# Feed-forward products of a two-layer trunk by Strassen's scheme over pairs of tiles

## The chip, the cores and the metric

The kernel runs on one core of one Trainium2 chip. TensorE (PE) multiplies matrices, VectorE (DVE), ScalarE (ACT) and GpSimd (POOL) work elementwise, and DMA queues, issued from SyncE (SP) or from GpSimd, move data between HBM and the on-chip memory SBUF. Products land in PSUM. The metric is device time in microseconds (us) of one execution.

## The reference

The reference is the trunk of a streaming encoder: 512 frames with 16 learned meta tokens in front, 1024 features, float32. Layer 0 is multi-scale retention, layer 1 multi-head latent attention with a shared compressed key and value; each layer ends with a dense feed-forward of hidden width 2816, with a norm ahead of each part and a residual addition behind it.

```python
def swiglu(hn, w1, w3, w2):
    return (jax.nn.silu(hn @ w1) * (hn @ w3)) @ w2

    for layer in range(DEPTH):
        hn = rmsnorm(h, norm_mix_g[layer])
...
        h = h + swiglu(rmsnorm(h, norm_ffn_g[layer]), ffn_w1[layer], ffn_w3[layer], ffn_w2[layer])
    return rmsnorm(h, final_g)[:, PAD + N_META:]
```

## The kernel before

Activations stay transposed: 128 features on the partitions of a tile, tokens along the free axis. The residual stream is eight tiles h0 to h7. A float32 product is three passes over operands split into an upper half (a cast on ACT) and a lower half (a subtraction on DVE); `split` (L212, L208) does it for weights as well as for activations, and `split_scaled` (L224, L225) together with a norm's gain.

The program runs in stages: retention (0 to 466 us), the feed-forward of layer 0 over 528 tokens (to 854), attention (to 1126), the feed-forward of layer 1 over 512 frames (to 1494), and an end. In a feed-forward (`ffn`), `gemm` walks over 44 tiles of 128 columns of w1 and w3 in turn, eight contraction tiles each, in two halves of 22; after each second tile `evac` scales both products by the norm's 1/rms, takes silu (L638), multiplies and splits the hidden tile. After each half, `gemm` multiplies eight columns of w2 with its eleven hidden tiles, and `add` adds the product to h. In the second half `add` also calls `prep`, which makes the next stage's operand from that h and sums its squares while the next tile's matmuls run. In layer 1 the second half of w2 is done by `finish`, for one half of the frames and then for the other, with the final norm and the output.

All operands live in one pool of 57 slots, and weights come through three buffers of raw, upper and lower halves (`wp`); PSUM has four buffers of two banks (1024 columns). On every engine instructions run in program order; the framework's scheduler has set that order from the code, and semaphores make each wait for its producers. GpSimd only issues transfers.

## Time and profile before

| what | before |
|---|---|
| median of 3 runs | 1505.89 us (1505.42 to 1507.55) |
| span of the profiled execution | 1505.8 us |
| its own time beside the span | not listed apart; the span lies within the runs' times |
| PE busy | 1486.9 us (99%) |
| DVE busy | 846.7 us (56%) |
| ACT busy | 571.0 us (38%) |
| POOL busy | 20.9 us (1%) |
| feed-forward stages | 466 to 854 and 1126 to 1494 us |

A busy share is that engine's own time over the span. Matmuls are pipelined, so a matmul's listed duration is longer than its distance to the next one; the chain of waits divides its length by their number.

### The profile page before, as it was taken

To read this page: it belongs to the slowest core of one execution; us is meant where nothing else is said; L and a number is where in the kernel's file an instruction comes from. 1 tells how busy PE (TensorE), PEld (TensorE's weight loads), DVE (VectorE), ACT (ScalarE), POOL (GpSimd) and SP (SyncE) were. 2 spreads that over 40 slices of the span, in tenths; PEclk is the share of its full clock that TensorE was granted. 3 is DMA by queue.
4 is the path that set the end of the run, shared out by engine and by line. 5 is a ranking of instruction groups with operands and counts; after the bars stand their busy time and mean duration, and the time that the engine had idled before them with its cause. 6 is when DMAs were issued, how large, how long until landed. Compare 5 with 4: busy or idle time off the path is not lost.

```text
span 1505.8 us, 24568 instructions
## 1 busy us (share of the span) xinstructions
PE 1486.9 (99%) x10450; PEld 1392.0 (92%) x10450; DVE 846.7 (56%) x1286; ACT 571.0 (38%) x946; POOL 20.9 (1%) x44
## 2 busy tenths in 40 slices
PE   8999999999999999999999999999999999999997
PEld 8999999999999999999999998889888888888896
DVE  7665565565577444234445667677885443344464
ACT  5452342342345222123224435666464222222251
POOL 1000000000000000000000000110000000000000
PEclk9999999999999999999999999999999999999998
DMA  5213213213212222332323422321113223323251
GB/s 202 88 47 111 80 46 110 80 48 109 70 58 94 89 88 70 96 112 86 95 67 87 139 84 80 103 67 67 57 44 111 98 81 88 112 98 98 81 160 57
DMA packets 43022, 133.91 MB, mean 89 GB/s; under 512 B 5136, under 2 KB 8720, under 8 KB 42912
## 3 DMA queue, kind: packets, MB, share of 16 engines
q1 hardware_dynamic: 40464, 125.98, 25.7%
q0 software_dynamic: 2448, 6.36, 1.5%
q8 instruction: 82, 1.34, 0.4%
q14 instruction: 28, 0.23, 0.0%
HBM read 128.91 MB, written 2.10 MB: 87 GB/s over the span
## 4 chain that ended last, share of the span: by engine, by line
PE 96%; DVE 1%; ACT 1%; DMA 0%; issue 0%; SPq 0%; DVEq 0%; ACTq 0%
PE ps L246 47%; PE ps L248 28%; PE ps L483 7%; PE ps L915 4%; PE ps L566 2%; PE ps L106 2%; PE ps L524 2%; PE ps L147 1%; PE ps L489 1%; PE ps L491 1%; PE ps L132 1%; PE ps L296 1%; DVE s L208 1%; ACT s L864 0%; DMA s<-w_q 0%; PE ps L567 0%
## 5 line engine op out<-in xcount | busy, mean ns | idle before, releaser
L246 PE MATMUL ps<-s,whi 128*128 128x264 f32 x3904 | 638.2, 285 | 6.5 <-ACT s L224 6.4
L246 PEld LDWEIGHTS ps<-s,whi 128*128 128x128 f32 x3904 | 543.4, 189 | 8.0 <-ACT s L224 6.8
L212 ACT CAST whi<-raw 128x1024 fp32r<-128x1024 f32 (+5 forms) x270 | 246.1, 917 | 652.3 <-PE ps L246 310.2
L246 PE MATMUL ps<-s,wlo 128*128 128x264 f32 x1952 | 398.4, 286 | 0.0
L248 PE MATMUL ps<-s,whi 128*128 128x512 f32 x1248 | 391.9, 395 | 0.5 <-DVE s L208 0.4
L208 DVE TENSOR_TENSOR wlo<-raw,whi 128x1024 fp32r<-128x1024 f32 (+5 forms) x270 | 284.3, 1056 | 107.2 <-ACT whi L212 104.7
L246 PEld LDWEIGHTS ps<-s,wlo 128*128 128x128 f32 x1952 | 303.8, 189 | 0.0
L248 PEld LDWEIGHTS ps<-s,whi 128*128 128x128 f32 x1248 | 232.4, 188 | 54.0 <-DVE s L208 1.0
L248 PE MATMUL ps<-s,wlo 128*128 128x512 f32 x624 | 244.8, 392 | 0.0
L208 DVE TENSOR_TENSOR t<-ps,s 128x528 f32<-128x528 f32 (+1 forms) x120 | 83.0, 700 | 279.8 <-PE ps L246 162.0
L248 PEld LDWEIGHTS ps<-s,wlo 128*128 128x128 f32 x624 | 117.1, 188 | 27.0
L208 DVE TENSOR_TENSOR h<-ps,h 128x528 f32<-128x528 f32 (+2 forms) x100 | 64.9, 653 | 93.3 <-PE ps L246 64.3
L483 PE MATMUL ps<-whi,s 128*128 128x256 f32 x640 | 116.0, 281 | 0.0
L208 DVE TENSOR_TENSOR s<-ps,s 128x256 fp32r<-128x256 f32 (+4 forms) x107 | 59.4, 571 | 89.9 <-ACT s L212 51.5
L483 PEld LDWEIGHTS ps<-whi,s 128*128 128x128 f32 x640 | 99.2, 189 | 0.2
L483 PE MATMUL ps<-wlo,s 128*128 128x256 f32 x320 | 89.7, 280 | 0.0
L483 PEld LDWEIGHTS ps<-wlo,s 128*128 128x128 f32 x320 | 60.4, 189 | 0.0
L212 ACT CAST s<-t 128x528 fp32r<-128x528 f32 (+2 forms) x68 | 40.2, 603 | 48.2 <-DVE t L208 39.4
L208 DVE TENSOR_TENSOR s<-s,s 128x528 fp32r<-128x528 f32 (+4 forms) x85 | 53.7, 657 | 4.9 <-ACT s L212 4.7
L212 ACT CAST s<-ps 128x256 fp32r<-128x256 f32 (+2 forms) x72 | 31.7, 445 | 61.0 <-PE ps L483 50.1
L208 DVE TENSOR_TENSOR s<-t,s 128x528 fp32r<-128x528 f32 (+2 forms) x68 | 44.5, 664 | 8.6 <-ACT s L212 8.4
L212 ACT CAST s<-s 128x528 fp32r<-128x528 f32 (+2 forms) x57 | 32.8, 584 | 39.8 <-DVE s L208 37.3
(140 smaller groups left out, 1105.1 us busy)
## 6 DMA issues: line engine op xcount, KB each, us to landing
raw<-w SPq DMA_DIRECT2D x99, 512.0 KB, 3.5
raw<-w SPq DMA_DIRECT2D x24, 384.0 KB, 3.1
raw<-w_v SPq DMA_DIRECT2D x16, 512.0 KB, 3.8
raw<-w_g SPq DMA_DIRECT2D x16, 512.0 KB, 3.4
raw<-w_ro SPq DMA_DIRECT2D x16, 512.0 KB, 3.4
raw<-w SPq DMA_DIRECT2D x24, 320.0 KB, 2.9
raw<-w_mo SPq DMA_DIRECT2D x8, 512.0 KB, 3.4
raw<-w_q SPq DMA_DIRECT2D x7, 512.0 KB, 4.2
```

Of the source, the lines that this page charges most:

```text
L106: nc.tensor.matmul(out, x[:, qs], y[:, cs], start=t == 0, stop=t == 4 and not masked)
L132: nc.tensor.transpose(pt[:, j * P : (j + 1) * P], p[:, META + j * P : META + (j + 1) * P], k.ident)
L147: nc.tensor.matmul(po[:, q0:SEQ], x, y, start=j == 0 and t == 0, stop=False)
L208: self.nc.vector.tensor_tensor(out=out, in0=a, in1=b, op=op)
L212: self.nc.scalar.copy(out=hi, in_=src)
L246: mm(ps[:, h * 512 : h * 512 + HT], w[p], x[q][:, h * HT : (h + 1) * HT], start=s, stop=e)
L248: mm(ps[:, :SEQ], w[p], x[q], start=s, stop=e)
L296: self.nc.tensor.matmul(ps[:, h * 512 : h * 512 + w], one, z[:, h * w : (h + 1) * w], start=i == 0, stop=i == len(acc) - 1)
L483: mm(ps[:, :256], x[k][p][:, c], w[k][q], start=k == 0 and i == 0, stop=k == last and i == 2)
L524: nc.tensor.matmul(ps[:n, half * 512 : half * 512 + HT], k[d][p][:, t0 : t0 + n], q[d][s][:, half * HT : (half + 1) * HT], start=i == 0, s ...
L566: mm(out, v[j][p][:, c], s[:, c0 : c0 + HT], start=j == 0 and i == 0, stop=False)
L915: nc.tensor.matmul(ps[:, :n], p, q, start=k == 0 and i == 0, stop=k == len(x) - 1 and i == 2)
```

## The change

Both feed-forwards are computed by the Strassen-Winograd scheme: two output tiles by two halves of the tokens, over pairs of contraction tiles, take seven products in place of eight. `quad` makes four output blocks, in four one-bank PSUM tiles, from seven factors of the weight and seven operands of the activation.

`factors` brings the four blocks of a weight and makes the sums: s3 and s1 by a plain transfer into SBUF followed by an accumulating one from GpSimd's queue, s2 and its second value by additions on DVE. All seven factors are split on ACT and DVE, 512 columns at a time. `operands` makes four differences on GpSimd and splits seven operands. The product of silu and gate is on GpSimd too. In `ffn`, a weight of w13 now has tile m of w1 and tile m of w3 side by side (22 up quads), and w2 comes in parts of 3, 3, 3 and 2 pairs of hidden tiles with four down quads each. Ahead of the down quads of the first three parts, one up quad of the next part is put.

The pools are opened and closed by stage, so that a stage's memory is free for the next. The preparation for attention now stands at the start of `mla`, that for layer 1's feed-forward after attention's pools are shut, and `finish` is replaced by the same down quads and a final norm over the whole frame. Weights of the other stages are split in pieces of 512. The order of some work between heads in attention is changed, too.

```diff
-SLOTS = 57
+WP = 512
+EW = 4 * HT
+RET_SLOTS = 45
+MLA_SLOTS = 53
+PARTS = (3, 3, 3, 2)
...
         self.retention()
-        self.ffn(0, True, self.prep_mla)
+        self.shut("pp", "yp")
+        self.hp = self.pool("hp", "right", 4)
+        self.ffn(0, True)
+        self.shut("hp", "wp")
+        self.weight_pool(2 * WP, 3, 6)
+        self.metas("mm", 4)
+        self.pp = self.pool("pp", bufs=4, space=PSUM)
+        self.sp = self.pool("sp", bufs=MLA_SLOTS)
         self.mla()
-        self.ffn(1, False, None)
+        self.shut("pp", "sp", "mm", "wp")
+        self.weight_pool(3 * WP, 2, 5)
+        self.xp = self.pool("xp", bufs=4)
+        self.hp = self.pool("hp", "right", 4)
+        for k in range(KD):
+            self.prep_ffn(1, k)
+        self.ffn(1, False)
...
     def prep_ffn(self, layer, k):
+        full = layer == 0
+        n = T if full else SEQ
+        v = self.h[k] if full else self.h[k][:, META:]
         if k == 0:
-            self.acc, self.x = self.slot(), []
-        self.x.append(self.prep(k, f"ffn{layer}", self.acc, layer == 0))
+            self.x = []
+        if k % 2 == 0:
+            self.vv = self.wide()[:, : 2 * n].rearrange("p (i c) -> p i c", i=2)
+        self.nc.scalar.activation(out=self.vv[:, k % 2], in_=v, func=AF.Copy, scale=self.g(f"ffn{layer}", k))
+        self.square_add(self.acc[:, :n], v, k == 0)
+        if k % 2:
+            self.x.append(self.operands(self.xp, self.vv, n // 2))
...
+    def operands(self, pool, vv, w):
+        nc = self.nc
+        add = nc.gpsimd.tensor_tensor
+        xp = pool.tile([P, 7, 2, HT], F32R, tag="xp", name=self.name("xp"))
+        tm = self.wide()[:, : 4 * w].rearrange("p (j c) -> p j c", j=4)
+        (b11, b12), (b21, b22) = ((vv[:, i, :w], vv[:, i, w : 2 * w]) for i in range(2))
+        add(out=tm[:, 2], in0=b12, in1=b11, op=ALU.subtract)
+        add(out=tm[:, 0], in0=b12, in1=b22, op=ALU.subtract)
+        add(out=tm[:, 1], in0=b22, in1=tm[:, 2], op=ALU.subtract)
+        add(out=tm[:, 3], in0=b21, in1=tm[:, 1], op=ALU.subtract)
+        self.split(xp[:, 0:2, 0, :w], xp[:, 0:2, 1, :w], vv[:, :, :w])
+        self.split(xp[:, 3:7, 0, :w], xp[:, 3:7, 1, :w], tm)
+        self.split_scaled(xp[:, 2, 0, :w], xp[:, 2, 1, :w], b22, -1.0)
+        return xp
+    def factors(self, src, n):
+        nc = self.nc
+        raw = self.raw()
+        s1, s2, s3 = (self.wp.tile([P, WP], F32, tag=t, name=self.name(t), bufs=1)[:, :n] for t in ("s1", "s2", "s3"))
+        nc.sync.dma_start(out=s3, in_=src[:, 3 * n : 4 * n])
+        nc.sync.dma_start(out=raw[:, : 3 * n], in_=src[:, : 3 * n])
+        nc.sync.dma_start(out=s1, in_=src[:, 3 * n : 4 * n])
+        nc.gpsimd.dma_start(out=s3, in_=src[:, :n], accum_op=ALU.add)
+        nc.gpsimd.dma_start(out=s1, in_=src[:, 2 * n : 3 * n], accum_op=ALU.add)
+        a11, a12, a22 = (raw[:, i * n : (i + 1) * n] for i in range(3))
+        for j, z in enumerate((a11, s3, s2, s1, a12, a22, s2)):
+            if j == 2:
+                self.tt(s2, s1, a11, ALU.add)
+            if j == 6:
+                self.tt(s2, s2, a12, ALU.add)
+            hi, lo = (t[:, :n] for t in self.ring())
+            self.split(hi, lo, z)
+            yield hi, lo
+    def quad(self, src, xs, w):
+        nc = self.nc
+        n = len(xs) * P
+        fac = self.factors(src, n)
+        ev = self.wide()[:, : 4 * w].rearrange("p (j c) -> p j c", j=4)
+        q1, u2, u3 = ev[:, 0], ev[:, 1], ev[:, 2]
+        def product(bank, j, first, last):
+            wt = next(fac)
+            for k, xp in enumerate(xs):
+                c = slice(k * P, (k + 1) * P)
+                for i, (p, q) in enumerate(((0, 0), (0, 1), (1, 0))):
+                    nc.tensor.matmul(bank[:, :w], wt[p][:, c], xp[:, j, q, :w], start=first and k == 0 and i == 0,
+                                     stop=last and k == len(xs) - 1 and i == 2, skip_group_check=True)
+        a, b, c, d = (self.bank() for _ in range(4))
+        product(a, 0, True, False)
+        nc.scalar.copy(out=q1, in_=a[:, :w])
+        product(d, 3, True, False)
+        product(b, 4, True, True)
+        self.tt(u2, b[:, :w], q1, ALU.subtract)
+        self.tt(u3, d[:, :w], u2, ALU.add)
+        product(c, 5, True, False)
+        c2 = self.temp()[:, : 2 * w]
+        self.tt(c2[:, w:], c[:, :w], u3, ALU.add)
+        product(a, 1, False, True)
+        product(d, 6, False, True)
+        self.tt(c2[:, :w], d[:, :w], u2, ALU.add)
+        product(c, 2, False, True)
+        self.tt(u3, c[:, :w], u2, ALU.add)
+        return a[:, :w], u3, c2
...
+        def up(m):
+            nonlocal vv
+            c11, c12, c2 = self.quad(a[f"w13_{layer}"][m], x, w)
+            if m == 0:
+                rstd()
+            c1 = self.temp()[:, :n]
+            self.tt(c1[:, :w], c11, r[:, :w], ALU.mult)
+            nc.vector.scalar_tensor_tensor(out=c1[:, w:], in0=c12, scalar=-1.0, in1=r[:, w:n], op0=ALU.mult, op1=ALU.mult)
+            self.tt(c2, c2, r[:, :n], ALU.mult)
+            nc.scalar.activation(out=c1, in_=c1, func=AF.Silu)
             if m % 2 == 0:
...
+                vv = self.wide()[:, : 2 * n].rearrange("p (i c) -> p i c", i=2)
+            nc.gpsimd.tensor_tensor(out=vv[:, m % 2], in0=c1, in1=c2, op=ALU.mult)
+            if m % 2:
+                hid.append(self.operands(self.hp, vv, w))
+        def down(part, xs, last):
+            for q in range(KD // 2):
+                c11, c12, c2 = self.quad(a[f"w2_{layer}_{part}"][q], xs, w)
+                h1, h2 = (z if full else z[:, META:] for z in self.h[2 * q : 2 * q + 2])
+                self.tt(h1[:, :w], c11, h1[:, :w], ALU.add)
+                self.tt(h1[:, w:], h1[:, w:], c12, ALU.subtract)
+                self.tt(h2, h2, c2, ALU.add)
+                if last and not full:
+                    for m in (2 * q, 2 * q + 1):
+                        self.square_add(acc, self.h[m][:, META:], m == 0)
+        m = 0
+        for part, size in enumerate(PARTS):
+            end = 2 * sum(PARTS[: part + 1])
+            ahead = 1 if part < len(PARTS) - 1 else 0
+            while m < end + ahead:
+                up(m)
+                m += 1
+            xs, hid[:] = hid[:size], hid[size:]
+            last = part == len(PARTS) - 1
+            if last:
+                self.shut("xp")
+            down(part, xs, last)
+        if not full:
+            rstd()
+            for k in range(KD):
+                hv = self.h[k][:, META:]
+                nc.vector.scalar_tensor_tensor(out=hv, in0=hv, scalar=self.g("final", k), in1=r[:, :n],
+                                               op0=ALU.mult, op1=ALU.mult)
+                nc.sync.dma_start(out=a["outT"][:, k], in_=hv)
+        self.shut("bk")
...
     def mla(self):
         nc, a = self.nc, self.a
+        for k in range(KD):
+            self.prep_mla(k)
         acc, xkv, xq = self.parted(self.acc, True), self.x, self.xq
-        r = self.slot()
+        r = self.r
...
-                if MH // 2 - 1 in pairs:
-                    self.prep_ffn(1, m)
```

The order of instructions, at three places. First GpSimd. Before, it holds nothing but DMA issues; these are the last of retention's decay tables and the first transfers of attention (ktrig, qtrig), with both feed-forward halves of layer 0 between decm_475 and s_1093.

```order
L415 DMA decm_321_2538<-decay_meta 16x528
L413 DMA dec_474_3796<-decay 128x656
L415 DMA decm_475_3798<-decay_meta 16x528
L666 DMA s_1093_9361<-ktrig 128x528
L669 DMA s_1094_9363<-qtrig 128x512
```

In the change, two up quads of layer 0's feed-forward stand on GpSimd as follows (s3 and s1 are weight sums, L806 the product of silu and gate into a pair's buffer e_884, L713 to L716 the differences for operand pair e_911).

```order
L731 DMA s3_920_6238<-w13_0 128x512
L806 TENSOR_TENSOR e_884_6075<-t_883_6070,t_876_6017 128x528
L713 TENSOR_TENSOR e_911_6219<-e_884_6075 128x264
L732 DMA s1_918_6236<-w13_0 128x512
L731 DMA s3_946_6380<-w13_0 128x512
L806 TENSOR_TENSOR e_884_6075<-t_909_6212,t_902_6159 128x528
L714 TENSOR_TENSOR e_911_6219<-e_884_6075 128x264
L715 TENSOR_TENSOR e_911_6219<-e_884_6075,e_911_6219 128x264
L716 TENSOR_TENSOR e_911_6219<-e_884_6075,e_911_6219 128x264
L732 DMA s1_944_6378<-w13_0 128x512
L731 DMA s3_973_6533<-w13_0 128x512
```

What moved: the products and differences are new there, and each accumulating transfer for s1 (L732) is issued only behind them. Next DVE, in the middle of layer 0's feed-forward. Before, it is the evacuation of one pair of product tiles (ps) by r (s_672), between lower halves of weights (wlo):

```order
L208 TENSOR_TENSOR t_882_7539<-ps_874_7429,s_672_5341 128x528
L208 TENSOR_TENSOR wlo_893_7607<-raw_891_7605,whi_892_7606 128x1024
L208 TENSOR_TENSOR t_883_7540<-ps_878_7484,s_672_5341 128x528
L208 TENSOR_TENSOR t_883_7540<-t_883_7540,t_882_7539 128x528
L208 TENSOR_TENSOR wlo_901_7672<-raw_899_7670,whi_900_7671 128x1024
L208 TENSOR_TENSOR s_885_7546<-t_883_7540,s_884_7545 128x528
L208 TENSOR_TENSOR t_894_7659<-ps_886_7549,s_672_5341 128x528
```

In the change, a stretch of the same stage (bk are PSUM banks, e_885 and e_912 combinations, c1 is t_909, xp_910 the operands of one pair):

```order
L245 TENSOR_TENSOR e_885_6077<-bk_888_6080,e_885_6077 128x264
L245 TENSOR_TENSOR wlo_928_6297<-s1_918_6236,whi_927_6296 128x512
L801 SCALAR_TENSOR_TENSOR t_909_6212<-e_885_6077,r_83 128x264
L245 TENSOR_TENSOR wlo_931_6315<-raw_917_6235,whi_930_6314 128x512
L245 TENSOR_TENSOR wlo_933_6331<-raw_917_6235,whi_932_6330 128x512
L245 TENSOR_TENSOR s2_919_6237<-s2_919_6237,raw_917_6235 128x512
L245 TENSOR_TENSOR xp_910_6218<-e_884_6075,xp_910_6218 128x2x264
L262 SCALAR_TENSOR_TENSOR xp_910_6218<-e_884_6075,xp_910_6218 128x264
L245 TENSOR_TENSOR e_912_6230<-bk_914_6232,e_912_6230 128x264
L245 TENSOR_TENSOR wlo_935_6349<-s2_919_6237,whi_934_6348 128x512
L245 TENSOR_TENSOR xp_910_6218<-e_911_6219,xp_910_6218 128x4x264
L245 TENSOR_TENSOR e_912_6230<-bk_916_6234,e_912_6230 128x264
```

What moved: combinations of banks and the subtractions for operand pairs now stand among the lower halves of weights, which have become halves of 512. Last DVE where layer 0's feed-forward meets attention. Before, the last two tiles' additions to h6 and h7, each followed by its operands (s_1074, s_1077, s_1086, s_1089) and its sum of squares (s_1001):

```order
L208 TENSOR_TENSOR h6_79<-ps_1066_9174,h6_79 128x528
L208 TENSOR_TENSOR wlo_1101_9380<-raw_1099_9378,whi_1100_9379 128x1024
L225 SCALAR_TENSOR_TENSOR s_1074_9255<-h6_79,gains_81,s_1073_9254 128x528
L208 TENSOR_TENSOR s_1001_8709<-s_1001_8709,t_1075_9258 128x528
L225 SCALAR_TENSOR_TENSOR s_1077_9262<-h6_79,gains_81,s_1076_9261 128x512
L208 TENSOR_TENSOR wlo_1107_9445<-raw_1105_9443,whi_1106_9444 128x1024
L208 TENSOR_TENSOR h7_80<-ps_1078_9265,h7_80 128x528
L208 TENSOR_TENSOR wlo_1113_9505<-raw_1111_9503,whi_1112_9504 128x1024
L225 SCALAR_TENSOR_TENSOR s_1086_9346<-h7_80,gains_81,s_1085_9345 128x528
L208 TENSOR_TENSOR s_1001_8709<-s_1001_8709,t_1087_9349 128x528
L225 SCALAR_TENSOR_TENSOR s_1089_9353<-h7_80,gains_81,s_1088_9352 128x512
L208 TENSOR_TENSOR s_1091_9357<-s_1001_8709,s_1090_9356 128x528
```

In the change the same place reads as follows, and goes on in this way through h7, sixteen scaled operands in all:

```order
L245 TENSOR_TENSOR h7_71<-h7_71,t_1766_10636 128x528
L245 TENSOR_TENSOR h6_70<-h6_70,e_1749_10578 128x264
L409 MEMSET meta_v0_1775_10683 80x512
L409 MEMSET meta_v1_1776_10684 80x512
L409 MEMSET meta_p0_1777_10685 80x528
L409 MEMSET meta_p1_1778_10686 80x528
L409 MEMSET xm_1779_10687 128x192
L262 SCALAR_TENSOR_TENSOR s_1783_10700<-h0_64,gains_72,s_1782_10699 128x528
L245 TENSOR_TENSOR acc_82<-acc_82,t_1793_10723 128x528
L262 SCALAR_TENSOR_TENSOR s_1785_10705<-h0_64,gains_72,s_1784_10704 128x512
L245 TENSOR_TENSOR acc_82<-acc_82,t_1798_10734 128x528
L262 SCALAR_TENSOR_TENSOR s_1787_10709<-h1_65,gains_72,s_1786_10708 128x528
```

What moved: five memsets and the preparation of all eight tiles h0 to h7 now stand behind the last addition to h6 and h7; before, they stood between the products of the last part.

## Rows read from the trace of the kernel before

**Rows 1.** The page's part 1: busy us, share, instructions of each engine.

```profile
PE 1486.9 (99%) x10450; PEld 1392.0 (92%) x10450; DVE 846.7 (56%) x1286; ACT 571.0 (38%) x946; POOL 20.9 (1%) x44
```

**Rows 2.** Chain that ended last, in order of time: start, length (us), line, count.

```profile
478.19 381.59 PE ps L246 x3120
...
860.27 23.29 PE ps L246 x192
...
1137.54 294.04 PE ps L248 x1272
1431.57 38.90 PE ps L915 x330
```

**Rows 3.** Table by stage: busy us (count) PE, PEld, DVE, ACT, POOL, clock, DMA share, GB/s.

```profile
466.00:854.00 388.00, 388.00 (x3174) 388.00 (x3174) 171.12 (x207) 116.43 (x150) 1.62 (x3) 1.00 0.29 91
1126.00:1494.00 368.00, 368.00 (x1852) 310.55 (x1851) 170.74 (x231) 113.07 (x159) 0.00 (x0) 1.00 0.31 98
1496.00:1506.00 10.00, 0.43 (x2) 0.03 (x1) 5.01 (x9) 0.47 (x1) 0.00 (x0) 0.58 0.31 105
```

**Rows 4.** Timeline of DVE at the retention stage's end: start, length.

```profile
455.26 1.23 DVE L208 TENSOR_TENSOR wlo<-raw,whi 128x1024 fp32r<-128x1024 f32 x1
456.40 0.76 DVE L225 SCALAR_TENSOR_TENSOR s<-h,gains,s 128x528 fp32r<-128x528 f32 x1
457.08 0.70 DVE L208 TENSOR_TENSOR s<-s,t 128x528 f32<-128x528 f32 x1
457.70 0.76 DVE L225 SCALAR_TENSOR_TENSOR s<-h,gains,s 128x528 fp32r<-128x528 f32 x1
```

**Rows 5.** Timeline of DVE near the end of attention.

```profile
1120.42 0.69 DVE L208 TENSOR_TENSOR s<-s,t 128x512 f32<-128x512 f32 x1
1121.02 0.75 DVE L225 SCALAR_TENSOR_TENSOR s<-h,gains,s 128x512 fp32r<-128x512 f32 x1
1121.68 0.69 DVE L208 TENSOR_TENSOR s<-s,t 128x512 f32<-128x512 f32 x1
```

**Rows 6.** Groups of DVE by form, 466 to 1506: busy us, mean ns, idle before.

```profile
L208 DVE TENSOR_TENSOR h<-ps,h 128x256 f32<-128x256 f32 x16 | 6.7, 420 | 10.7 <-PE ps L915 10.6
...
L308 DVE RECIPROCAL s<-s 128x512 f32<-128x512 f32 x2 | 6.7, 3348 | 0.8 <-ACT s L306 0.8
...
L208 DVE TENSOR_TENSOR wlo<-raw,whi 128x384 fp32r<-128x384 f32 x6 | 3.3, 556 | 4.1 <-ACT whi L212 4.0
```

**Rows 7.** Groups of ACT by form, 466 to 1506.

```profile
L212 ACT CAST whi<-raw 128x1024 fp32r<-128x1024 f32 x113 | 118.5, 1050 | 340.1 <-issue 139.3 <-PE ps L246 100.5 <-PE ps L248 99.3
...
L638 ACT ACTIVATE t<-t 128x528 f32<-128x528 f32 x22 | 14.0, 643 | 0.4 <-DVE t L208 0.4
...
L224 ACT ACTIVATE s<-h,gains 128x512 fp32r<-128x512 f32 x16 | 11.4, 713 | 5.4 <-DVE h L208 5.4
...
L212 ACT CAST whi<-raw 128x512 fp32r<-128x512 f32 x12 | 6.8, 618 | 10.7 <-PE ps L248 4.0 <-issue 4.0 <-DMA raw<-w 1.6
```

**Rows 8.** Groups of POOL, whole span.

```profile
L415 POOL DMA_DIRECT2D decm<-decay_meta x4 | 2.0, 508 | 6.1 <-DVE t L536 4.3 <-DMA h<-xT 1.8
```

**Rows 9.** DMA issues: KB each, median us from issue to landing.

```profile
raw<-w SPq DMA_DIRECT2D x99, 512.0 KB, 3.5
...
s<-ktrig POOLq DMA_DIRECT2D x1, 264.0 KB, 3.0
```

**Rows 10.** Timeline of DVE at the span's start.

```profile
1.19 1.03 DVE L326 MEMSET meta_v<- 80x512 f32 x2
2.28 1.06 DVE L326 MEMSET meta_p<- 80x528 f32 x2
```

**Rows 11.** Timeline of the span's end, all engines.

```profile
1494.29 0.42 DVE L208 TENSOR_TENSOR h<-ps,h 128x256 f32<-128x256 f32 x1 [2.47 <-PE ps L915]
...
1496.98 1.75 DVE L883 RECIPROCAL s<-s 128x256 f32<-128x256 f32 x1 [1.30 <-ACT s L882]
1498.77 3.25 DVE L886 SCALAR_TENSOR_TENSOR h<-h,gains,s 128x256 f32<-128x256 f32 x8
```

More of the change, by code (lines that the diff above doesn't have):

```diff
@@ L55, in drain, with __init__, __getitem__ @@
         pass
+class Pieces:
+    def __init__(self, tiles):
+        self.tiles = tiles
+    def __getitem__(self, key):
+        rows, c = key
+        i = c.start // WP
+        return self.tiles[i][rows, c.start - i * WP : c.stop - i * WP]
 class Filler:
@@ L134, in weights @@
         ptv = pt[:, : (i + 1) * P].rearrange("p (j q) -> p j q", q=P)
-        k.split(self.ph[:, : i + 1, qs], self.pl[:, : i + 1, qs], ptv)
+        for j in range(0, i + 1, 2):
+            js = slice(0, min(2, i + 1 - j))
+            k.split(self.ph[j // 2][:, js, qs], self.pl[j // 2][:, js, qs], ptv[:, j : min(j + 2, i + 1)])
         k.stacked(self.pm[:, qs], pt[:META, 512 : 512 + P], 64)
@@ L644, in add @@
-        def add(m, ps):
-            hv = self.two(self.h[m]) if full else self.h[m][:, META:]
-            self.tt(hv, self.view(ps, full), hv, ALU.add)
-            if part:
-                prep(m)
-        for part in range(2):
-            hid.clear()
-            up = self.gemm(a[f"w13_{layer}"], part * KH, KH, x, full, evac=evac,
-                           mid=None if part else partial(self.rstd, r, acc, D, self.eps_rms[:, 0:1], full),
-                           mid_at=1)
-            drain(up)
-            if part and not prep:
-                self.finish(a[f"w2_{layer}"][part], hid)
-            else:
-                drain(self.gemm(a[f"w2_{layer}"][part], 0, KD, list(hid), full, chunk_k=6, evac=add))
+        vv = None
@@ L929, in _blocks, with _pair @@
         w.reshape(k // P, P, m // cols, cols).transpose(2, 1, 0, 3)).reshape(m // cols, P, k // P * cols)
+def _pair(w1, w2):
+    half = [z.reshape(-1, 2, P, P).transpose(1, 2, 0, 3).reshape(2, P, -1) for z in (w1, w2)]
+    return np.ascontiguousarray(np.concatenate([half[0][0], half[0][1], half[1][1], half[1][0]], 1))
 def _angles(dim):
@@ L971, in _arrays @@
     for n in range(2):
-        w1, w3 = _blocks(i["ffn_w1"][n]), _blocks(i["ffn_w3"][n])
-        a[f"w13_{n}"] = np.ascontiguousarray(np.stack([w1, w3], 1)).reshape(2 * KH, P, D)
-        a[f"w2_{n}"] = np.stack([_blocks(z) for z in np.split(i["ffn_w2"][n], 2)])
+        w1, w3, w2 = i["ffn_w1"][n], i["ffn_w3"][n], i["ffn_w2"][n]
+        cols = lambda z, m: z[:, m * P : (m + 1) * P]
+        a[f"w13_{n}"] = np.stack([_pair(cols(w1, m), cols(w3, m)) for m in range(KH)])
+        k = 0
+        for part, size in enumerate(PARTS):
+            rows = w2[k : k + 2 * size * P]
+            k += 2 * size * P
+            a[f"w2_{n}_{part}"] = np.stack([_pair(cols(rows, m), cols(rows, m + 1)) for m in range(0, KD, 2)])
     wk = i["mla_w_kv_a"]
```

187 lines of the change are left out of this document (82 added, 105 removed).

## The prediction

> **What bounds the kernel now.** I read the page's busy line first [rows 1]: the matrix engine (PE) is busy 1486.9 us of 1505.8, VectorE (DVE) 846.7, ScalarE (ACT) 571.0, GpSimd (POOL) 20.9. A share over the whole span hides the stages, so next the chain of waits [rows 2]: in both feed-forward stages it is nothing but matmuls, in runs of 381.59 us and 294.04 us without a break. The table by stage [rows 3] says the same: from 466 to 854 PE is busy all 388 us and DVE 171, ACT 116; from 1126 to 1494 it is 368, 171 and 113, at a granted clock of 1.00 throughout. So in these 756 us the time is the number of matmuls times their cadence, and DVE stands at 44 to 46%. What matters is how many matmuls go, and whether the work that replaces them still fits behind PE.
>
> **Term 1, the matmuls removed.** A feed-forward is now 22 up quads of 7 products over 4 pairs of tiles and 4 down quads for each of the parts of 3, 3, 3 and 2 pairs (11 pairs in all), each product three passes: 22 x 7 x 4 x 3 + 4 x 7 x 11 x 3 = 2772 matmuls of 264 columns (layer 0) or 256 (layer 1). Before it was 3168 of 264 columns in layer 0. The cadence at 264 is 381.59 / 3120 = 0.1223 us, and at 256 it is 38.90 / 330 = 0.1179 [rows 2]. Layer 0: 2772 x 0.1223 = 339.0 against 387.9, so -48.9. Layer 1: 2772 x 0.1179 = 326.8 against 368.2, so -41.4. Together **-90.3**.
>
> **Term 2, DVE beside it.** The lower halves of the operands, the sums for factors and the combinations of products land on DVE. Its price back to back is the distance of two starts, which is about 0.08 under the listed duration: 0.62 for 528 columns (457.08 to 457.70), 0.68 for a scalar form of 528 (456.40 to 457.08), 1.14 for 1024 [rows 4], 0.60 for 512 (1120.42 to 1121.02) and 0.66 for its scalar form (1121.02 to 1121.68) [rows 5]. By that 0.08, the 384-column subtraction (556 ns) costs 0.48 and the 256-column one (420 ns) 0.34 [rows 6]; 264 columns I take at 0.35, their scalar form at 0.40. An up quad of layer 0 has seven lower halves and two sums of 512 (9 x 0.60 = 5.4), five combinations of 264 (1.7), then 0.35 + 0.40 + 0.62 for the scaling: 8.5. The operands of two quads (528, 4 x 264 and a scaled 264) cost 0.62 + 1.18 + 0.40 = 2.2, so 9.6 a quad, where PE needs 84 x 0.1223 = 10.3. A down quad of three pairs: 9 x 0.48 + 1.7 + 1.3 = 7.3 against 63 x 0.1223 = 7.7; of two pairs 9 x 0.34 + 1.7 + 1.3 = 6.1 against 42 x 0.1223 = 5.1. In sum DVE has 324 us against PE's 339 in layer 0; likewise 325 against 327 in layer 1, where the last four quads also add squares (7.2 against 4.9). So DVE rises from 44% to 96 and 99% of the stage: what was cover is used up. ACT has 7 casts of 512, a silu and its copies, some 5.4 to 6 a quad of 10.3 at 0.62 and 0.64 [rows 7], and isn't the bound. The last down quads are DVE's own: 4 x 1.0 and 4 x 2.3, **+13**.
>
> **Term 3, the new path through GpSimd.** In the rows of order, after the second quad of a pair POOL multiplies silu and gate, makes three more differences, and only behind them issues the accumulating transfer for the next quad's s1. DVE runs in order: the scaled combination (L801) stands three weight instructions (1.8 us) ahead of the subtraction that makes xp's lower half, which waits on silu (0.64), POOL's product and ACT's cast (0.62) [rows 7]. Behind that wait stand the combinations that free PSUM banks and the lower halves that PE takes next. No row of before shows arithmetic on POOL: its rows are issues of some 0.5 us [rows 8]. From below, it runs as DVE does (0.70 for 528): 0.64 + 0.70 + 0.62 is about what lies between, and the loss is nothing. At twice that the chain is late by some 0.9 a pair of quads, 22 pairs, +20. Nearest is the DVE row of the same shape, the slope to a slower engine unknown; I take half, 0.45 a pair, **+10**, with 0 and the first rival's price as ends. The page GPSIMD Engine Reference of the Trainium skill (section 4.1 Engine selection, with the table of 3.1) says to keep elementwise adds and products on VectorE, GpSimd being 1.96 times slower; no run here shows it yet, and by it the term would be the +20.
>
> The transfers themselves: a POOL-queue transfer of 264 KB lands 3.0 us after issue and 512 KB of weights 3.5 [rows 9]. An up quad reads seven blocks of 256 KB, two of them accumulating, in 10.3 us: 1.8 MB, twice the 91 GB/s at which the DMA share is 0.29 [rows 3]. For s3 the issue is a quad ahead: nothing. For s1 it is behind POOL's differences; from there to DVE's first sum lie six DVE instructions, about 3 us, so it just fits. An accumulation dearer than a plain transfer is the third rival.
>
> **Term 4, the start of the last part.** There no up quad runs ahead of the down quads, so the last operands are on the path: combination 0.42, scalar form 0.48, silu 0.64, product 0.70, three differences of 0.42, cast of 1056 columns 1.1 and its lower half 1.2: 5.8 a layer, **+11**. With POOL at twice the price 7.8.
>
> **Term 5, retention to layer 0.** The last pair of operands takes the same chain without product and silu, some 3 us more than the split it replaces: **+3** (0 to 5).
>
> **Term 6, layer 0 to attention.** Before, each tile's normalised copies, squares and sums stood between the products of the last part (the block of order on h6 and h7 before), and PE went from 859.78 to 860.27, a gap of 0.5 [rows 2]. Now all of it comes after the last h. DVE does: two combinations and adds 1.4, four memsets (two in 1.03 and two in 1.06 [rows 10]) and a small one 2.3, sixteen scalar forms at 0.66 to 0.68 (10.7), six sums 3.7, seven lower halves of weights 4.2: 22.3 us, before the first product can end, since it needs all eight tiles. PE has 48 matmuls in it, 5.9. **+16** (12 to 20).
>
> **Term 7, attention to layer 1.** The preparation of the eight tiles, interleaved before, now waits for memory that the last attention matmuls read. After these ACT has four pairs' casts (0.62 + 1.05 + 0.45 each, 8.5), the last pair's scaled copies (0.71) and squares (taken as silu's 0.64), twice: 2.7 [rows 7], and four weight casts at 0.52 back to back; with POOL's and DVE's share at the end of the chain (4) that is some 17 us until four products have run, which are 48 x 0.1179 = 5.7. **+11** (6 to 15).
>
> **Term 8, the end.** Before, the span ends 11.5 us after DVE takes up the last product (1494.29): final sum, matmuls, a reciprocal of 1.75 on 256 columns, eight scalar forms in 3.25, output [rows 11]. Now the whole frame: reciprocal 3.35 [rows 6], eight at 0.66 (5.3), two combining steps more (0.6) and squares and transfers twice as wide (0.7): **+5**.
>
> **Term 9, the clock.** Where PE stood idle at the end (1496 to 1506, busy 0.43 of 10) the granted clock reads 0.58 [rows 3]. After the two starved stretches of terms 6 and 7 some matmuls may run at the lower of its two levels (1.2 instead of 2.4 GHz), half as fast; 48 of them would lose 5.9: **+3**, 0 to 8.
>
> **Sum:** -90.3 + 13 + 10 + 11 + 3 + 16 + 11 + 5 + 3 = -18. The profiled execution's span is 1505.8, against a median of 1505.89 of the runs (1505.42 to 1507.55), so nothing to speak of lies outside it: 1505.9 - 18 = **1488 us**. 0.2%, 3 us, is about what these runs can tell from no change.
>
> **Rivals.** *POOL and DVE get in each other's way (slower).* If POOL's arithmetic and DVE's two-operand instructions on SBUF can't run at once, POOL's time is added to DVE's. A pair of quads has two products and four differences: at twice DVE's price 2 x 1.25 + 4 x 0.65 = 5.1. Of DVE's 19.3 a pair some 14 (73%) are such instructions, so DVE gets 19.3 + 3.7 = 23.0 against PE's 20.5: +2.5 a pair in place of 0.45, 22 pairs, +45: 1533 (1564 if all of POOL's time counts, about 1500 at DVE's price). It decides from 1.27 us a pair. For it: DVE has no slack left (term 2). Against it: in the rows of before POOL does no arithmetic, so none shows it. The Trainium skill speaks for it in SBUF — State Buffer, section Who interferes with whom: a VectorE instruction with two SBUF inputs contends with a GpSimd instruction that reads SBUF, and the later one is blocked. No run here shows it yet.
>
> *The boundaries are mostly hidden (faster still).* If POOL costs nothing, DVE does not fall behind in the last quads, and half of the boundary work overlaps: terms 2 to 9 become 8 + 0 + 5 + 1 + 8 + 6 + 5 + 0 = 33: 1449. For it: PE's 99% now shows that the order of work hides such things well. Against: the instruction order puts them after the last h.
>
> *Accumulating transfers land late (slower).* If one takes 6 us instead of 3, DVE waits 3 us at the sum in each second quad, 22 x 3 = +66: 1554. From 0.8 us a pair on top of the 0.45 the gain is gone. For it: no such transfer in the trace of before; against: twice a DMA share of 0.29 leaves room [rows 3].
>
> **Chances.** Main case 0.42, by its terms 1470 to 1503; hidden boundaries 0.17 (1440 to 1470); the engines' conflict 0.26 (1500 to 1564); late transfers 0.10; 0.05 for what I don't see, and the cases' edges. Main and hidden give 0.55 faster, with the part of the main case that ends near zero taken off; 0.08 for within 0.2%; 0.37 slower, from both slow rivals and the rest. The range takes the hidden case and most of the conflict, 1446 to 1545; the likeliest alone is 1470 to 1503.
>
> **What would show it.** PE: 2772 matmuls a layer at the old cadence. DVE near 95% in the stage, its longest waits on ACT's xp cast (behind POOL) and on s1's transfer. PE idle at the two changes of stage, 16 and 11 us. POOL's product of 528 near 0.7 to 1.4. It is wrong if DVE's subtractions of 512 grow above 0.69 while POOL works (conflict), if DVE waits for the transfers, or if PE stays above 97% within layers and less than half is lost at the boundaries.

## The result and the profile after

The changed kernel takes 1799.69 us (median of 4 runs, 1797.14 to 1800.97) against 1505.76 beside it: the ratio is 1.1947, interval 1.193 to 1.1964. It is slower by 294 us, where 18 us less was forecast.

The page's busy line and its line on the chain by engine, of the changed kernel:

```profile
PE 1522.1 (85%) x10980; PEld 1444.8 (80%) x10980; DVE 1306.2 (73%) x2369; ACT 755.3 (42%) x1539; POOL 339.6 (19%) x360
...
PE 46%; DVE 20%; DMA 16%; POOL 7%; ACT 6%; issue 5%; DVEq 0%; ACTq 0%; SPq 0%; POOLq 0%
```

PE's busy time rose, by 35 us [rows 1]. Its instructions rose in number, too, because layer 1's matmuls, partly of 512 columns before, are all of 256 now; in layer 0, where the width stayed, they fell from 3168 to 2772. The chain, which was matmuls alone in the feed-forward stages [rows 2], is 46% PE now, with DVE, DMA and POOL in it. The table by stage (columns as in [rows 3]; cut at the first and the last feed-forward matmul of each layer):

```profile
466.00:478.80 12.80, 2.12 (x18) 1.93 (x17) 10.52 (x14) 6.96 (x13) 5.89 (x6) 0.75 0.20 42
478.80:975.80 497.00, 398.88 (x2776) 381.78 (x2776) 380.28 (x682) 187.33 (x371) 147.22 (x145) 0.90 0.49 119
975.80:1287.40 311.60, 278.66 (x1670) 242.66 (x1668) 229.82 (x486) 173.18 (x407) 24.11 (x34) 0.95 0.24 72
1287.40:1778.80 491.40, 385.41 (x2775) 366.39 (x2776) 378.28 (x685) 184.72 (x371) 141.73 (x143) 0.91 0.49 119
1778.80:1797.30 18.50, 2.00 (x7) 0.95 (x5) 11.65 (x15) 3.38 (x5) 0.00 (x0) 0.62 0.30 114
```

Layer 0 takes 497.0 us from its first to its last product against 388 before, layer 1 491.4 against 368; that is 232 of the 292 us between the spans. The rest lies ahead of layer 0 (12.8), between the layers (311.6, against 272 from 854 to 1126) and in the end (18.5 against 11.5). In the layers DVE is busy 380 of 497, so no engine is full: something waits in turn. The granted clock is 0.90 there, against 1.00 [rows 3]. Two of the waits over the whole span (waiting instruction, releaser, total us, times, longest):

```profile
DVE s L245 <- DMA s<-w: 125.4, 47, 5.1
PE bk L757 <- ACT whi L249: 124.6, 56, 11.4
```

Two links in that chain are worth reading. First, a stretch of down quads, in which GpSimd computes nothing. The chain in order of time (start, length, what):

```profile
602.28 5.14 DMA s<-w
...
607.51 0.56 DVE s L245
...
609.76 1.48 DVE wlo L245 x3
...
613.22 5.30 DMA s<-w
...
618.61 0.56 DVE s L245
```

and the issues of s1's transfers in the same stretch, accumulating on GpSimd (L732) and plain on SP's queue (L730):

```profile
602.28 0.86 POOL L732 DMA_DIRECT2D s<-w  x1 [4.15 <-DVE h L245]
...
613.22 0.86 POOL L732 DMA_DIRECT2D s<-w  x1 [4.62 <-DVE wlo L245]
```

```profile
610.33 0.33 SPq L730 DMA_DIRECT2D s<-w  x1
```

The order of the changed kernel lets s1's plain transfer start only when its only buffer's last reader, the previous quad's lower half, is done; the accumulating one starts behind it. At 607.51 DVE's sum starts, behind an accumulation issued at 602.28 that took 5.14 us; at 609.76 the lower halves behind it run, at 610.33 the plain transfer for the next quad goes out, at 613.22 its accumulation, and at 618.61 the next sum: 11.1 us from sum to sum, where PE has 7.7 us of work. (The row of 613.22 names an instruction of DVE as the one that ended GpSimd's wait; the plain transfer sent at 610.33 lands about then, too: such transfers of 192 KB take 3.0 us at the median.) GpSimd's arithmetic has no part in this loop.

Second, the second up quad of a pair, in the same view:

```profile
645.38 0.56 ACT t L803
...
646.01 1.40 POOL e L806
...
647.48 1.08 POOL e L714
648.56 1.15 POOL e L715
...
649.80 1.09 POOL e L716
...
650.91 1.08 ACT xp L249
...
652.01 1.26 DVE xp L245
...
653.67 4.55 PE bk L757 x24
```

From silu to the lower half of the operands 7.9 us pass (645.38 to 653.27), 4.9 of them on GpSimd, and PE then runs 24 matmuls in 4.55 us, 0.19 each instead of 0.1223. The table by stretch around this shows why (columns as in [rows 3]):

```profile
649.10:653.60 4.50, 0.02 (x1) 0.00 (x0) 3.99 (x7) 2.63 (x4) 2.52 (x3) 0.96 0.68 205
653.60:656.40 2.80, 2.73 (x12) 2.73 (x13) 2.49 (x6) 0.00 (x0) 0.00 (x0) 0.50 0.26 45
656.40:660.00 3.60, 3.60 (x31) 3.60 (x30) 2.79 (x6) 2.00 (x4) 0.35 (x1) 0.96 0.27 77
```

After 4.5 us with hardly a matmul the granted clock is 0.50 for 2.8 us, the lower of its two levels (1.2 GHz), and then mostly the upper again (2.4 GHz). DVE's share shows by forms (columns as in [rows 6]), with GpSimd's own and the transfers' beside them:

```profile
L245 DVE TENSOR_TENSOR wlo<-raw,whi 128x512 fp32r<-128x512 f32 x320 | 237.6, 758 | 53.2 <-ACT whi L249 52.8
...
L245 DVE TENSOR_TENSOR s<-s,raw 128x512 f32<-128x512 f32 x88 | 82.8, 940 | 71.5 <-DMA s<-w 71.3
...
L245 DVE TENSOR_TENSOR e<-bk,e 128x264 f32<-128x264 f32 x114 | 48.5, 425 | 8.3 <-PE bk L757 7.6
...
L245 DVE TENSOR_TENSOR xp<-e,xp 128x528 fp32r<-128x528 f32 x15 | 16.6, 1110 | 5.2 <-ACT xp L249 4.6
```

```profile
L732 POOL DMA_DIRECT2D s<-w x76 | 65.9, 867 | 176.2 <-DVE wlo L245 70.8 <-DVE t L245 35.2 <-DVE h L245 32.3
...
L806 POOL TENSOR_TENSOR e<-t,t 128x528 f32<-128x528 f32 x22 | 35.1, 1596 | 35.0 <-ACT t L803 35.0
```

```profile
s<-w SPq DMA_DIRECT2D x88, 256.0 KB, 3.5
s<-w POOLq DMA_DIRECT2D x88, 256.0 KB, 4.3
```

A subtraction of 512 costs 0.758 on the mean (of all stages) and a sum 0.940, where [rows 5] had 0.69, and the operand's lower half of 528 1.110 against 0.70 [rows 4]; the combinations that read a bank of PSUM keep their 0.425 (0.42 in [rows 6] for 256 columns). GpSimd's product of 528 takes 1.596.

### The profile page after: what moved, and what is told of

Read it like the earlier page. It is cut to its first block, busy times and chain, and to the rows that moved or that the text cites. A ratio compares the mean times of both kernels' runs of the same rounds, so it can differ in the third digit from the quotient of the medians.

```text
span 1797.3 us, 28613 instructions
## 1 busy us (share of the span) xinstructions
PE 1522.1 (85%) x10980; PEld 1444.8 (80%) x10980; DVE 1306.2 (73%) x2369; ACT 755.3 (42%) x1539; POOL 339.6 (19%) x360
## 4 chain that ended last, share of the span: by engine, by line
PE 46%; DVE 20%; DMA 16%; POOL 7%; ACT 6%; issue 5%; DVEq 0%; ACTq 0%; SPq 0%; POOLq 0%
PE ps L294 16%; DMA s<-w 15%; PE bk L757 10%; DVE wlo L245 7%; PE ps L296 7%; PE ps L568 5%; DVE s L245 4%; DVE e L245 3%; ACT whi L249 2%; POOL e L806 2%; PE ps L651 2%; DVE t L245 2%; POOL e L715 2%; PE ps L125 1%; ACT xp L249 1%
## 5 line engine op out<-in xcount | busy, mean ns | idle before, releaser
L757 PE MATMUL bk<-xp,whi 128*128 128x264 f32 (+1 forms) x3696 | 751.3, 304 | 206.8 <-ACT whi L249 124.6
L757 PEld LDWEIGHTS bk<-xp,whi 128*128 128x128 f32 x3696 | 625.8, 207 | 230.4 <-ACT whi L249 146.2
L757 PE MATMUL bk<-xp,wlo 128*128 128x264 f32 (+1 forms) x1848 | 554.2, 303 | 19.4 <-DVE wlo L245 18.8
L757 PEld LDWEIGHTS bk<-xp,wlo 128*128 128x128 f32 x1848 | 377.4, 205 | 32.5 <-DVE wlo L245 31.4
L245 DVE TENSOR_TENSOR wlo<-raw,whi 128x512 fp32r<-128x512 f32 (+3 forms) x444 | 295.0, 682 | 56.4 <-ACT whi L249 55.7
L249 ACT CAST whi<-raw 128x512 fp32r<-128x512 f32 (+3 forms) x444 | 246.9, 571 | 210.4 <-PE ps L294 126.4
L294 PE MATMUL ps<-s,whi 128*128 128x264 f32 x1792 | 295.9, 287 | 12.2 <-ACT s L261 6.4
L294 PEld LDWEIGHTS ps<-s,whi 128*128 128x128 f32 x1792 | 251.4, 191 | 14.4 <-ACT s L261 6.4
L294 PEld LDWEIGHTS ps<-s,wlo 128*128 128x128 f32 x896 | 140.6, 191 | 8.0 <-DVE wlo L245 8.0
L296 PE MATMUL ps<-s,whi 128*128 128x512 f32 x368 | 117.5, 400 | 1.6 <-DVE s L245 1.6
L713 POOL TENSOR_TENSOR e<-e 128x264 f32<-128x264 f32 (+1 forms) x30 | 31.3, 1044 | 392.4 <-ACT e L430 391.2
L732 POOL DMA_DIRECT2D s<-w x76 | 65.9, 867 | 176.2 <-DVE wlo L245 70.8
```

The costliest lines, as they stand in the source:

```text
L245: self.nc.vector.tensor_tensor(out=out, in0=a, in1=b, op=op)
L249: self.nc.scalar.copy(out=hi, in_=src)
L294: mm(ps[:, h * 512 : h * 512 + HT], w[p], x[q][:, h * HT : (h + 1) * HT], start=s, stop=e)
L296: mm(ps[:, :SEQ], w[p], x[q], start=s, stop=e)
L713: add(out=tm[:, 2], in0=b12, in1=b11, op=ALU.subtract)
L732: nc.gpsimd.dma_start(out=s1, in_=src[:, 2 * n : 3 * n], accum_op=ALU.add)
```

## The experiments

Ten kernels, each a change to the changed kernel; "floor" is the fifth of them, with neither of the two suspects, transfers and GpSimd's arithmetic. The first four take these singly and together. The scheduler sets the order of the instructions anew for each kernel, so two kernels can differ in more than their edit. On DVE in layer 0 four have nearly the same order: the floor, the run with GpSimd beside it, and the runs with the arithmetic on DVE and one or three buffers for s1. Most other pairs have not.

Two buffers for each sum:

```diff
-        s1, s2, s3 = (self.wp.tile([P, WP], F32, tag=t, name=self.name(t), bufs=1)[:, :n] for t in ("s1", "s2", "s3"))
+        s1, s2, s3 = (self.sm.tile([P, WP], F32, tag=t, name=self.name(t))[:, :n] for t in ("s1", "s2", "s3"))
...
+        self.sm = self.pool("sm", "right", 2)
```

> Two buffers each for the weight sums s1, s2 and s3 in place of one, from a pool of their own; GpSimd's arithmetic stays. Theory A (with one buffer each, the next quad's plain transfer, the accumulating one behind it, the sum, split and product stand one behind another and set the quad's period): the down quads of three pairs, which the trace of the change shows every 11 to 12 us on the accumulating queue against 7.7 us of matmuls, fall to about 8, and the time to 1560 to 1660 us. Rival B (GpSimd's arithmetic is slow and holds DVE up): the down quads, which have no arithmetic on GpSimd, can't be explained by it, and the time stays above 1740.

Measured: 1704.21. Neither figure held, since neither cause is alone. In layer 0 most down quads of three pairs fall to 7.5 to 7.8 us, as theory A said; the up quads of the part behind them stay at 14.3 us on the mean (14.5 in the changed kernel), where PE needs 10.3.

No accumulations:

```diff
-        nc.gpsimd.dma_start(out=s3, in_=src[:, :n], accum_op=ALU.add)
-        nc.gpsimd.dma_start(out=s1, in_=src[:, 2 * n : 3 * n], accum_op=ALU.add)
```

> The two accumulating transfers of each quad are left out, so s1 and s3 hold one block each and the sums are incomplete; buffers stay single, the plain transfers stay. Theory A: the chain loses 4.3 us of transfer and 0.87 of issue per quad, 76 quads, and the time falls by 200 to 330 to 1470 to 1600. Rival B: the conflict is still there in all up quads; under it alone the time stays above 1740.

Measured: 1622.33, 177 less and just above the range. Transfers are the larger part, and something is left that they don't explain.

Arithmetic on DVE:

```diff
-        add = nc.gpsimd.tensor_tensor
+        add = nc.vector.tensor_tensor
...
-            nc.gpsimd.tensor_tensor(out=vv[:, m % 2], in0=c1, in1=c2, op=ALU.mult)
+            nc.vector.tensor_tensor(out=vv[:, m % 2], in0=c1, in1=c2, op=ALU.mult)
```

> Silu's product and the four differences run on DVE in place of GpSimd; single buffers and accumulating transfers stay. Theory A: DVE gets about 1.3 us a quad more, the down quads keep their 11 to 12 us, and the time lies between 1700 and 1800. Rival B: the period of the up quads falls to DVE's load, about 11 us, and the time to about 1650 or less. Rival C (the accumulating transfers are held behind GpSimd's arithmetic, and it behind their waits, on one queue): a gain of some 1 to 3 us an up quad, 44 of them, 1670 to 1750.

Measured: 1736.27, inside the figures of theory A and of rival C, which it doesn't tell apart. DVE has more to do and the time falls by 63, so GpSimd's arithmetic costs more than it takes off DVE; but the single buffers stay the larger matter.

Both edits:

> Both: two buffers for the sums, and the product and differences on DVE. Theory A with B or C as the rest: PE or DVE sets the period, 10.3 to 11 us an up quad and 7.7 a down quad; the sum of the forecast without its third term, plus 1.3 us of DVE in 44 quads less its slack, is 1480 to 1540. If the time stays above 1600, the cause is in neither, and the transfers themselves (DMA share 0.5) would be next.

Measured: 1607.60, above 1600: by its own condition a further cause. Its second quads of a pair still took some 16 us in places, with DVE waiting for s1. Four more kernels follow that.

The floor (no accumulations, arithmetic on DVE; s1 and s3 in two buffers, s2 in one):

> Neither of the two: GpSimd's arithmetic on DVE, and the accumulating transfers left out, so that s1 and s3 hold one block each and the sums are incomplete. What is left is DVE at some 10.9 us an up quad (9.6 and 1.3 moved there), PE at 10.3, and the changes of stage. If the two causes (transfers, GpSimd's arithmetic) explain the loss: 1490 to 1530. If it stays above 1560, a third cause is at work in all versions.

Measured: 1586.94. The condition for a third cause holds. The layers take 390.0 and 389.9 us, with DVE busy 362 and 361.

GpSimd beside the floor:

```diff
+        if pool is not self.xp:
+            for i in range(4):
+                nc.gpsimd.tensor_tensor(out=self.scr[:, :w], in0=b12, in1=b11, op=ALU.subtract)
...
+            nc.gpsimd.tensor_tensor(out=self.scr[:, :n], in0=c1, in1=c2, op=ALU.mult)
```

> As the floor, with the same number of GpSimd instructions on the same inputs beside it (one product a quad, four differences a pair), which write a scratch tile that nobody reads: nothing waits for their results. Conflict of the two engines over SBUF: VectorE's subtractions of 512 beside them grow from 0.69 to over 1.2 us, and the time by 2 to 4 us a pair of quads, 22 pairs: +45 to +90 over the floor. If GpSimd costs only by its slowness and by what is queued behind it, the time is that of the floor to within 10 us.

Measured: 1690.33, 103 over the floor and above the range, from instructions whose results nobody reads. No wait of PE, DVE or ACT in this run was ended by GpSimd, so it isn't their reading of the same buffers that holds the others up. DVE is busy 404 and 408 us in the layers, 88 more than in the floor. The down quads, beside which GpSimd computes nothing, keep their time (9.0 and 8.5 us). DVE's forms in the floor, and then in this run:

```profile
L245 DVE TENSOR_TENSOR wlo<-s,whi 128x512 fp32r<-128x512 f32 x176 | 120.0, 687 | 19.3 <-ACT whi L249 19.1
...
L245 DVE TENSOR_TENSOR e<-bk,e 128x264 f32<-128x264 f32 x114 | 48.7, 428 | 2.7 <-PE bk L755 2.1
...
L245 DVE TENSOR_TENSOR xp<-e,xp 128x528 fp32r<-128x528 f32 x15 | 10.5, 703 | 0.0
```

```profile
L245 DVE TENSOR_TENSOR wlo<-s,whi 128x512 fp32r<-128x512 f32 x176 | 144.3, 825 | 18.2 <-ACT whi L249 18.1
...
L245 DVE TENSOR_TENSOR e<-bk,e 128x264 f32<-128x264 f32 x114 | 48.4, 425 | 4.7 <-PE bk L758 4.5
...
L245 DVE TENSOR_TENSOR xp<-e,xp 128x528 fp32r<-128x528 f32 x15 | 14.3, 954 | 0.0
```

Forms with two operands in SBUF grow, from 687 to 825 ns and from 703 to 954 on the mean; the combination with one operand in PSUM does not. GpSimd's product on 528 columns takes 2.3 us on the mean here, against 1.6 in the changed kernel:

```profile
L811 POOL TENSOR_TENSOR scr<-t,t 128x528 f32<-128x528 f32 x22 | 50.1, 2275 | 626.3 <-ACT t L807 626.3
```

Three buffers for s1 (shown against the run with both edits):

```diff
-        s1, s2, s3 = (self.sm.tile([P, WP], F32, tag=t, name=self.name(t))[:, :n] for t in ("s1", "s2", "s3"))
+        s1, s2, s3 = (self.sm.tile([P, WP], F32, tag=t, name=self.name(t), bufs=b)[:, :n] for t, b in (("s1", 3), ("s2", 1), ("s3", 2)))
```

> As the run with both edits (two buffers, arithmetic on DVE), with three buffers for s1, two for s3 and one for s2. If the time to free a buffer still sets when s1's transfers start, the second quads of a pair fall from 16 to 11.5 us and the time from 1608 to 1540 to 1570. If the transfers are late through their own queue (the accumulations wait one behind another on GpSimd, and take up to 8 us beside the weights), it stays at 1590 or more.

Measured: 1587.86, the time of the floor: with three buffers the accumulations cost nothing more, although one of 256 KB lands 5.8 us after issue at the median. Neither figure expected held, because the floor was not known. Layer 0 in the table by stage, and the chain through the slow half of a pair:

```profile
478.60:870.10 391.50, 366.70 (x2776) 348.76 (x2776) 362.04 (x753) 183.32 (x368) 62.16 (x73) 0.99 0.59 147
```

```profile
632.77 0.63 ACT whi L249
...
633.42 0.69 DVE wlo L245
...
640.29 0.43 DVE t L245
...
641.43 0.63 ACT whi L249
...
642.62 13.44 PE bk L757 x106
```

PE runs 106 matmuls in a row, and in between the chain goes for eight microseconds through DVE's instructions one behind another, from 633.42 to 641.3. It came back 23.6 us later in the same form, where PE needs 20.5 for the pair. DVE is busy 362 of 391 us. ACT's casts wait for DVE's sums in between:

```profile
ACT whi L249 <- DVE s L245: 87.0, 54, 4.4
```

All sums on DVE, without accumulations, each in one buffer (the lines taken out are not shown):

```diff
+        nc.sync.dma_start(out=raw[:, : 4 * n], in_=src)
+        a11, a12, a22, a21 = (raw[:, i * n : (i + 1) * n] for i in range(4))
...
+            if j == 1:
+                self.tt(s3, a21, a11, ALU.add)
             if j == 2:
+                self.tt(s1, a21, a22, ALU.add)
                 self.tt(s2, s1, a11, ALU.add)
```

> No accumulating transfer and no arithmetic on GpSimd: all four sums and all differences and products on DVE, weights in one plain transfer of four blocks. DVE then needs 9.6 + 1.3 + 1.2 = 12.1 us an up quad and 8.3 a down quad of three pairs, so it is the bound: 22 x 12.1 + 12 x 8.3 + 4 x 6.8 = 393 us a layer, 787 against 756 before, and with 40 to 50 us at the changes of stage and the end 1575 to 1590. If waits and not loads were the matter, it would be nearer to 1520.

Measured: 1625.38, 37 over the run before and 35 to 50 above what the load alone gave. DVE is busy 398 of 412 us in layer 0 and 399 of 409 in layer 1, so its own work is nearly all of the time here, somewhat more than the 393 reckoned, and waits add 10 to 13 us a layer.

The last two kernels ask whether DVE's load is the floor, and whether buffers alone, with the arithmetic still on GpSimd, cure the transfers. First, without the sums for s2:

```diff
-        for j, z in enumerate((a11, s3, s2, s1, a12, a22, s2)):
-            if j == 2:
-                self.tt(s2, s1, a11, ALU.add)
-            if j == 6:
-                self.tt(s2, s2, a12, ALU.add)
+        for j, z in enumerate((a11, s3, s1, s1, a12, a22, a12)):
```

> As the run with three buffers for s1 and the arithmetic on DVE, without DVE's two sums for s2 in each quad (the third and the seventh factor take s1 and a12 in their place, so these sums are left out). DVE loses 22 x 1.2 + 12 x 0.96 + 4 x 0.68 = 41 us a layer, from 353 to 312, below PE's 339 and 327. If DVE's load is what the rest of the loss in the layers comes from, a layer falls from 391 to 350 and the time from 1588 to 1505 to 1520. If the in-order waits of DVE on ACT, the five ring buffers or the order of products set the pace, the time stays above 1560.

Measured: 1508.66, inside the range for DVE's load. The table by stage, and a run of matmuls in layer 0 (412 in 50.53 us, 0.1226 each):

```profile
466.00:478.60 12.60, 7.43 (x41) 7.24 (x41) 11.01 (x21) 5.82 (x10) 0.85 (x1) 0.63 0.33 108
478.60:836.40 357.80, 348.64 (x2776) 344.04 (x2776) 327.94 (x677) 197.71 (x368) 62.28 (x73) 0.99 0.64 160
836.40:1142.90 306.50, 277.48 (x1669) 241.63 (x1667) 229.63 (x496) 173.66 (x409) 12.24 (x23) 0.97 0.25 78
1142.90:1489.30 346.40, 338.16 (x2776) 333.25 (x2776) 324.48 (x678) 197.43 (x369) 62.57 (x73) 0.99 0.67 166
1489.30:1507.60 18.30, 2.31 (x7) 1.21 (x5) 11.71 (x15) 3.38 (x5) 0.00 (x0) 0.59 0.30 115
```

```profile
646.84 50.53 PE bk L753 x412
```

Layer 0 falls to 357.8 and layer 1 to 346.4, with PE busy 349 and 338: the layers are PE's again, and 52 us below those of before, and the time is still that of before, since the changes of stage and the end cost 54 more than before (12.6 ahead of layer 0, 306.5 against 272, 18.3 against 11.5). The edit takes out more than load: the waits of ACT's casts for DVE's sums, 87 us in layer 0 of the run before, are gone as well, and the order of DVE's instructions is another.

Second, the buffers alone:

> Three buffers for s1, two for s3 and one for s2, with the arithmetic still on GpSimd. If, with two buffers (1704), it was still the transfers that came late because buffers came free late, the time falls to that without accumulations, 1620 to 1640. If the accumulations are late because they stand on one queue with GpSimd's arithmetic and wait behind it (and it behind them), the time stays near 1700.

Measured: 1636.42, as the first of the two theories had it. DVE's sums of 512 columns, which waited 71.5 us for transfers in the changed kernel, now wait 1.0:

```profile
L245 DVE TENSOR_TENSOR s<-s,raw 128x512 f32<-128x512 f32 x88 | 87.3, 992 | 1.0 <-DMA s<-w 1.0
```

This run also shows that a full DVE need not cost PE anything. Three down quads of layer 0 in it, and three in the run with three buffers and the arithmetic on DVE (columns as in [rows 3]):

```profile
579.40:601.70 22.30, 22.30 (x185) 22.30 (x184) 22.04 (x52) 10.75 (x24) 3.47 (x5) 1.00 0.80 193
```

```profile
674.00:700.00 26.00, 24.98 (x191) 23.51 (x190) 23.08 (x54) 11.59 (x27) 4.31 (x5) 1.00 0.74 187
```

The work of a down quad is the same in both, since none of the arithmetic that was moved lies there. In the first run PE never stops, with DVE busy 99%; in the second a quad takes 1.2 us more, with DVE busy 89%. The two runs without accumulations show the same, 7.5 us against 9.0 and 8.5, so the transfers aren't it. What the traces show to differ is the order: in the second run ACT's copy of a bank (L762), which waits for PE, and three more of DVE's instructions stand ahead of the sum and the casts that the next products need. A run that changes the order alone was not made.

The times side by side (us). With two buffers all three sums have two; with three, s1 has three, s3 two and s2 one. The last row leaves accumulations out, with one buffer each on GpSimd's side, and two for s1 and s3 on DVE's:

| buffers for s1 | arithmetic on GpSimd | on DVE |
|---|---|---|
| one | 1799.7 | 1736.3 |
| two | 1704.2 | 1607.6 |
| three | 1636.4 | 1587.9 |
| no accumulation | 1622.3 | 1586.9 |

No version with complete sums beat the kernel before; the best takes 1587.9.

## Why the prediction was wrong

**Terms 1 and 2's loads were right.** The matmul count is 2772 a layer, and in the run without s2 they run at the old cadence (0.1226 us against 0.1223). DVE at the floor is busy 362 us a layer; my sum with the arithmetic moved there is 324 + 22 x 1.3 = 353, worked out from back-to-back starts.

**The step that failed first is in term 3: "For s3 the issue is a quad ahead: nothing. For s1 ... it just fits."** I read the place of the issue in GpSimd's order and took what it waits for as done. s1 and s3 have one buffer each; plain transfer (3.5), issue (0.87) and accumulation (4.3) start only when the last quad's reader is done, and DVE waits for them in order (these are the medians at 256 KB). More buffers alone take 163 us off (1799.7 to 1636.4), all but 14 of what leaving the accumulations out does. The late transfers were my third rival, at 0.10 and +66: the side was right, the mechanism not. A transfer need not be dear for it; at 4.3 us against the 3.0 that I took it is only a little so, and at 5.6 in the run with three buffers it cost DVE about 1 us in all. The diff shows bufs=1, and I did not follow what that frees, when. DVE's wait for the transfers was one of the signs that I had named for being wrong.

**The other half of term 3, the wait behind silu, was too short.** I counted silu, one product and a cast, some 2 us. The cast that DVE waits for stands behind the three differences, too: the trace has 7.9 us from silu to the lower half, 4.9 of them on GpSimd, where I charged 0.45 a pair of quads.

**The conflict of the engines is shown; its share in the changed kernel is not.** It had 0.26 and +45. Moving the arithmetic to DVE, which by itself adds 1.3 us a quad to the fuller engine, takes 63 us off with one buffer, 97 with two, 49 with three and 35 without accumulations (there the buffers differ, too). These are nets of conflict, latency, DVE's added load and another order, so that 49 is near 45 is no test of the rival's sum. The run with GpSimd instructions that nobody waits for beside the floor sets the conflict apart from queue and latency: +103, with DVE busy 88 us longer on the same number of instructions. The sign that I had named, subtractions of 512 above 0.69 while POOL works, came as well. The rule that the Trainium skill gives in SBUF — State Buffer (Who interferes with whom), that a VectorE instruction with two SBUF inputs contends with a GpSimd instruction that reads SBUF, agrees with this trace: 687 ns become 825, and a form that reads PSUM stays at 425 to 428. The Trainium skill's GPSIMD Engine Reference (3.1 Elementwise — side-by-side cycle accounting) has 1.96 for the ratio of the two engines on a sum; here the product of 528 took 1.596 against 0.70, 2.3 times, beside a working DVE.

**Term 2's conclusion failed: a share of 96 to 99% was taken as covered.** I charged only the last down quads (+13). With neither transfers nor GpSimd in the way, a layer takes 390 where the longer of PE (339) and DVE (353) would give 353, and without the sums for s2 it takes 358 and 346: 79 us in both layers. That is the price of these sums, and not of their 41 us of load alone: layer 1 falls by 45, ACT's waits for them go as well, and the order changes. A DVE as full as PE was cover after all in the down quads of the run with three buffers and the arithmetic on GpSimd (22.04 of 22.30 us, PE without a stop), and was not in another order of the same work (26.00). In the up quads with the arithmetic on DVE its load is above PE's (21.8 against 20.5 a pair, by the prices of term 2), and they take 23.6. So term 2 put at nothing what an in-order engine loses when it waits for PE and ACT and PE for it; how much of the 79 is load and how much order was not tried.

**Terms 6 to 9 were right in kind and somewhat small.** Forecast 16 + 11 + 3 between the layers: measured 311.6 - 272 = 40, and 34 to 38 in the runs with the arithmetic on DVE. The end: 5 forecast, 7 measured. Term 5 was mis-sized, 3 against 12.8, of which PE waits 10.7 in one stretch ahead of the layer's first matmul. With the differences on DVE the layer still starts 12.6 late, but PE then waits elsewhere: 7.1 us ahead of retention's last product, for a lower half that stands behind the differences. With all sums on DVE it starts 8.8 late. So what sets it stays open. Term 4 can't be told apart in these runs.

**Term 9's clock was placed wrongly.** I charged it at the two changes of stage only. In the changed kernel the stalls inside the layers lower it, to a mean of 0.90, and PE is busy 399 us with matmuls that take 339 at the full level. With most of the stalls gone (0.99 and 0.97 in the run with three buffers and the arithmetic on DVE) it came back, so some of what each edit gave is clock; how much was not set apart.

So the layers came out 232 us over in place of 56 under (terms 1 to 4). Undone one after another, the single buffers give 163 us, GpSimd's arithmetic 49, and the sums for s2 79; the two layers then take 704 us, where the forecast had 756 - 56 = 700. Undone in another order the shares are others, and the last step leaves out work that the result needs, so that 704 is near 700 is no sign that the forecast could be reached.

## What to carry to other kernels

A transfer that is issued early in an order helps only if its buffer is free early: for each one, look for the last reader of the buffer before it, and add its latency to that reader's time. Saving an eighth of the bounding engine's matmuls by filling the next engine to the same height gave nothing back here: two in-order engines that wait for one another then hang on the order of their instructions, and the same work cost nothing in one order and 1.2 us a quad in another. So look at that order before taking a full engine for cover. And arithmetic put on GpSimd was paid for on VectorE where both read SBUF: +103 us from instructions that nobody waited for.
